# 256-byte alignment, several weight layouts and backward reads in a float32 encoder block

## The chip, the cores and the metric

The kernel runs on one core of one Trainium2 chip. The metric is the device time of one execution in microseconds (us), taken as the median of several runs. A core has five engines that run side by side: TensorE (PE in the profile; its weight loads are PEld), VectorE (DVE), ScalarE (ACT), GpSimd (POOL) and SyncE (SP), which here issues DMAs. They meet through semaphores. Operands lie in SBUF, which has 128 partitions; TensorE writes its results to PSUM.

## The reference

One layer of an encoder block on 512 tokens of width 1024, in float32. Cut to what matters:

```python
h = rms_norm(x, mix_norm_g)
proj = h @ w_in          # mLSTM q,k,v,o,gates | neighbourhood attention q,k,v | memory q | merge gates
y_ml = mlstm_branch(...)             # bidirectional, 4 heads of 128
y_na = neighbourhood_attention(...)  # 8 heads of 64 on an 8 x 64 grid
y_xa = memory_cross_attention(...)   # 4 heads of 128, 256 memory tokens
merged = g_ml * (y_ml @ w_br_ml) + g_na * (y_na @ w_br_na) + g_xa * (y_xa @ w_br_xa)
x = x + merged @ w_out
a, u = split(rms_norm(x, ffn_norm_g) @ w_ffn_up)     # 1024 -> 2 x 2816
x = x + (gelu(dwconv3(a, w_ffn_conv, b_ffn_conv)) * u) @ w_ffn_down
return rms_norm(x, final_norm_g)
```

## The kernel before

Activations are kept with channels on the partitions and the 512 tokens along the free axis. Every large product is done in three matmuls: each operand is split into a high part of type fp32r, a rounded float32, and a low part, which is what is left. `mm3` (L201 to L204) adds high x high (L202), high x low (L203) and low x high (L204) into one PSUM bank. In most products the stationary operand is a 128 x 128 tile of weights and the moving one 128 x 512 of activations; each matmul loads its weights anew.

Weights come in blocks, in one fixed order, `BLOCKS`. `emit_raw` (L141 to L151) starts the DMA of a block into one of three raw buffers, `raw`. `emit_split` (L167 to L188) splits it half by half: ACT copies to the high tile `wh` (L184), DVE subtracts to get the low tile `wl` (L185). There are four buffers for high and four for low tiles, each 544 words wide (`HWD`), so two blocks of two halves fit. `weights` (L190 to L199) hands out a block and sees to it that raw blocks are three ahead and splits one ahead.

`proj` (L332 to L340) is one product over eight steps of k, that is 24 matmuls, into one PSUM bank. The order of stages: mLSTM q and k, the token-major values (256 or 272 columns, activations stationary), memory q and output gates, memory k and v, neighbourhood q and k, then the three branches with their merge gates, with the attention work (generators advanced by `step`) interleaved; then the output projection `out` (activations `GH`, `GL`), and the feed-forward network in two halves of 11. In each half 11 tiles f are made: `ua` (the part that goes through convolution and GELU) and `uu` (the factor), each one block of 8 x 128 columns and 24 matmuls; activations are `HH` and `HL`. Blocks `dn` then do the down projection.

Activations lie in `unit` tiles of 2064 words (`UNIT`), four slices of 512 to a unit; there are 15 of them. Scratch tiles (`scr`) are 516 words wide. Pools lie behind one another: constants, then `wp` (raw, high, low), then the units. Where a tile starts, modulo 256 bytes, follows from these widths.

Of the kernel before, what the change touches and what calls it, by code (L numbers as in the profile page):

```python
# [11 lines left out]
F32 = mybir.dt.float32  # L12
F32R = mybir.dt.float32r
AF = mybir.ActivationFunctionType
ALU = mybir.AluOpType
AX = mybir.AxisListType

P = 128
S = 512
D = 1024  # L20
KT = D // P
# [11 lines left out]
NEG = -1e30  # L33
BW = 1088
HWD = 544
UNIT = 2064
ROWS, GW = 8, 64
CW = (0, 8, 24, 32)
C_ML = (128.0 ** -0.5) / 4.0
# [44 lines left out]
    return L  # L84


BLOCKS = block_list()
BINDEX = {}
_off = 0
# [12 lines left out]
def hybrid_block(ctx, tc, xT, memT, wflat, vecs, gbias, nabias, outa, outb):  # L102
# [14 lines left out]
    def nm(s):  # L117
        uid[0] += 1
        return f"{s}_{uid[0]}"
# [2 lines left out]
        return up.tile([P, UNIT], dt, tag="unit", name=nm("u"))  # L122

    def scr(n=512):
        return sp.tile([P, 516], F32, tag="scr", name=nm("s"))[:, :n]

    def tiny(n):
        return tp.tile([P, 32], F32, tag="tiny", name=nm("y"), bufs=12)[:, :n]
# [8 lines left out]
    raws, split = {}, {}  # L137
# [14 lines left out]
    def halves(i):  # L152
# [2 lines left out]
        k0 = k if n <= HWD else (k + 1) // 2  # L155
        return c, [(0, k0)] + ([(k0, k)] if k0 < k else [])

    lw = []

    def lastw(k, m):  # L160
# [6 lines left out]
    def emit_split(i):  # L167
        key, n = BLOCKS[i]
        r = raws.pop(i)
        c, hs = halves(i)  # L170
        split[i] = []
        for a, b in hs:
            m = (b - a) * c
            if key[0] == "dnl":
                h, l = lastw(4 * key[1] + a, m)
            else:
                h = wp.tile([P, HWD], F32R, tag="hi", name=nm("wh"), bufs=4)
                l = wp.tile([P, HWD], F32R, tag="lo", name=nm("wl"), bufs=4)
            for u, v in ((0, P), (P, m)) if i == 0 and a == 0 else ((0, m),):
                src = r[:, a * c + u:a * c + v]  # L180
                if i == 0 and a == u == 0:
                    V.tensor_copy(h[:, u:v], src)
                else:
                    A.activation(h[:, u:v], src, AF.Copy)  # L184
                V.tensor_tensor(l[:, u:v], src, h[:, u:v].bitcast(F32), op=ALU.subtract)  # L185
            for k in range(a, b):
                q = slice((k - a) * c, (k - a + 1) * c)
                split[i].append((h[:, q], l[:, q]))  # L188

    def weights(key):  # L190

# [17 lines left out]
        V.scalar_tensor_tensor(l, src, scale, h.bitcast(F32), op0=ALU.mult, op1=ALU.subtract)  # L209


    vec = cp.tile([P, NVEC], F32, name="vec")
    gb = cp.tile([P, 16], F32, name="gb")

# [75 lines left out]
    def rstd_row(col, ntok, tag):  # L290

        nt = ntok // P
        ch, cl = tp.tile([P, 32], F32R, tag="tiny", name=nm("y"), bufs=12)[:, :nt], tiny(nt)
        A.activation(ch, col, AF.Copy)
        V.tensor_tensor(cl, col, ch.bitcast(F32), op=ALU.subtract)
        pb = atps()
        for n, c in enumerate((ch.bitcast(F32), cl)):
            dg = sp.tile([P, 516], F32R, tag="scr", name=nm("s"))[:, :ntok]
            for t in range(nt):
                V.tensor_scalar(dg[:, t * P:(t + 1) * P], ident, c[:, t:t + 1], None, op0=ALU.mult)  # L300
            PE.matmul(pb[:, :ntok], onesr, dg, start=n == 0, stop=n == 1)
        rb = cp.tile([P, ntok], F32, name=f"rb_{tag}", tag=f"rb{ntok}", bufs=2 if ntok == S else 1)
        A.activation(rb, pb[:, :ntok], AF.Copy)
        return rb
# [27 lines left out]
    def proj(key, XHs, XLs, n=S, bank=None, at={}):  # L332
        ws = weights(key)
        ps = (bank or mmps)()
        for k in range(KT):
            mm3(ps[:, :n], ws[k][0], ws[k][1], XHs[k], XLs[k], k == 0, k == KT - 1)
            if k in at:
                at[k]()
        return ps
# [73 lines left out]
    for c in range(4):  # L413
        n = 272 if c == 0 else 256
        pss = [(mmps if c % 2 else atps)() for _ in range(NT)]
        for h in range(2):
            ws = weights(("tm", c, h))
            for t in range(NT):
                tsl = slice(t * P, (t + 1) * P)
                for k in range(4):  # L420
                    kk = 4 * h + k
                    ps = pss[t][:, :n]
                    mm3(ps, XH[kk][:, tsl], XL[kk][:, tsl], ws[k][0], ws[k][1], kk == 0, kk == KT - 1)
        for t in range(NT):
            ps = pss[t]
            if c == 0:
                V.scalar_tensor_tensor(Gt[:, t, :], ps[:, :16], rc[:, t:t + 1], gb, op0=ALU.mult, op1=ALU.add)
            if c < 2:
                o = 16 if c == 0 else 0
                A.activation(va[:, t, 2 * c:2 * c + 2, 0:128],  # L430
                             ps[:, o:o + 256].rearrange("p (h c) -> p h c", h=2), AF.Copy, scale=rcc[:, t:t + 1])
            else:

                nv = sp.tile([P, 516], F32R, tag="scr", name=nm("nv"))[:, :512]
                nvv = nv.rearrange("p (q y d) -> p q y d", q=2, y=4)
                pv = ps[:, :256].rearrange("p (q e d) -> p q e d", q=2, e=2)
                A.activation(nvv[:, :, 0:4:3, :], pv, AF.Copy, scale=rc[:, t:t + 1])
                for q in range(2):
                    V.scalar_tensor_tensor(nvv[:, q, 1:3, :], pv[:, q], rc[:, t:t + 1], nvv[:, q, 0:4:3, :].bitcast(F32),
                                           op0=ALU.mult, op1=ALU.subtract)  # L440
                G.dma_start(nav_d[t * P:(t + 1) * P, (c - 2) * 512:(c - 1) * 512], nv)
# [329 lines left out]
    def xa_all(xq, mk, mv, yh, yl):  # L771
        rt = lambda: tp.tile([P, S], F32R, tag="R", name=nm("X"), bufs=4)
        vv = lambda a: a.rearrange("p (m c) -> p m c", m=2)

        def prep(h):
            q, k = (rt(), rt()), rt()
            split_act(q[0], q[1], xq[:, h * S:(h + 1) * S])
            k = (k[:, :M], k[:, M:])
            split_act(k[0], k[1], mk[:, h * M:(h + 1) * M])
            return q, k  # L780

        def prep_v(h):
            v = rt()
            v = (v[:, :M], v[:, M:])
            split_act(vv(v[0]), vv(v[1]), vv(mv)[:, :, h * P:(h + 1) * P])
            return v

        def scores(tq, q, k):
            ps = atps()
            for i in range(2):  # L790
                t = 2 * tq + i
                tsl = slice(t * P, (t + 1) * P)
                mm3(ps[:, i * M:(i + 1) * M], q[0][:, tsl], q[1][:, tsl], k[0], k[1], True, True)
            mx = tiny(2)
            psv = ps.rearrange("p (a b) -> p a b", a=2)
            V.tensor_reduce(mx, psv, axis=AX.X, op=ALU.max, negate=True)
            V.tensor_scalar(mx, mx, XSC, None, op0=ALU.mult)
            sm = scr()
            su = tiny(2)
            for i in range(2):  # L800
                A.activation(sm[:, i * M:(i + 1) * M], psv[:, i, :], AF.Exp, scale=XSC, bias=mx[:, i:i + 1],
                             accum_out=su[:, i:i + 1])
            V.reciprocal(su, su)
            for i in range(2):
                V.tensor_scalar(sm[:, i * M:(i + 1) * M], sm[:, i * M:(i + 1) * M], su[:, i:i + 1], None, op0=ALU.mult)
            return sm

        def transposes(tq, sm, pT):
            pt = atps()
            for i in range(2):  # L810
                for hf in range(2):
                    PE.transpose(pt[:, (2 * hf + i) * P:(2 * hf + i + 1) * P],  # L812
                                 sm[:, i * M + hf * P:i * M + (hf + 1) * P], ident)
            for hf in range(2):
                ms = slice(tq * M, (tq + 1) * M)
                split_act(pT[hf][0][:, ms], pT[hf][1][:, ms], pt[:, hf * M:(hf + 1) * M])

        def values(h, v, pT):
            py = atps()
            for hf in range(2):  # L820
                vs = slice(hf * P, (hf + 1) * P)
                mm3(py, v[0][:, vs], v[1][:, vs], pT[hf][0], pT[hf][1], hf == 0, hf == 1)
            hs = slice(h * S, (h + 1) * S)
            split_act(yh[:, hs], yl[:, hs], py)

        q, k = prep(0)
        yield
        prev = None
        for h in range(4):
            sm = [scores(tq, q, k) for tq in range(2)]  # L830
            if prev:
                values(h - 1, *prev)
            yield
            v = prep_v(h)
            pT = [[sp.tile([P, 516], F32R, tag="scr", name=nm("s"))[:, :S] for _ in range(2)] for _ in range(2)]
            for tq in range(2):
                transposes(tq, sm[tq], pT)
            prev = (v, pT)
            if h < 3:
                q, k = prep(h + 1)  # L840
            yield
        values(3, *prev)
        yield
# [423 lines left out]
```

## Time and profile before

| | |
|---|---|
| three runs | 904.84, 904.88 and 905.72 us, median 904.88 us |
| the profiled execution, first to last instruction | 902.3 us |
| that to the median of the runs | 2.6 us lie outside the span |
| PE busy | 894.4 us (99%), 4438 matmul records |
| PEld busy | 749.2 us (83%) |
| DVE, ACT, POOL busy | 597.7, 464.9, 157.0 us |
| granted TensorE clock, mean | 0.998 |

The page gives for each engine the busy time and its share of the span; the profiled execution's own time is this span and what lies around it, before the first and behind the last instruction. A group of instructions has its line, engine, operation, tiles and shapes, its count, busy time in us and the mean in ns of one, and behind the second bar the idle time before it. [...]

### The profile page before, as it was taken

The page shows a single profiled execution, that of the slowest core. Times are in us where ns is not written, and L with a number is a line of the kernel's source. Part 1 is how long each engine was busy: PE and PEld are TensorE (multiplying, and loading weights), DVE is VectorE, ACT ScalarE, POOL GpSimd, SP SyncE. Part 2 cuts the span into 40 slices and gives each one's busy share as a digit, 9 for nine tenths or more (in the row PEclk, how much of TensorE's full clock was granted, in tenths as well). Part 3 has the DMA queues.
Part 4 walks back from the last instruction along what each step waited for, and adds up shares of the span by engine and source line. Part 5 has one row for each costly group of instructions (what it writes and reads, how often), then busy time and mean ns, then how long its engine had stood idle before and what let it go on. Part 6 is the DMA issues. An engine that isn't in the chain of part 4 may idle for free.

```text
span 902.3 us, 12444 instructions
## 1 busy us (share of the span) xinstructions
PE 894.4 (99%) x4438; PEld 749.2 (83%) x4438; DVE 597.7 (66%) x1138; ACT 464.9 (52%) x982; POOL 157.0 (17%) x236
## 2 busy tenths in 40 slices
PE   9999999999999999999999999999999999999997
PEld 7899888888888888888888888888888888888887
DVE  6795577746566757998766657777733477777433
ACT  7474456656544646898734435444422344444432
POOL 4201231102070660420000211111100011111010
PEclk9999999999999999999999999999999999999999
DMA  8224633422252443443323432222133322222412
GB/s 265 94 76 131 193 134 104 164 94 94 70 136 76 116 126 120 135 135 118 117 88 107 134 108 96 94 98 94 65 99 95 116 94 94 94 93 89 137 33 94
DMA packets 39437, 99.69 MB, mean 110 GB/s; under 512 B 5960, under 2 KB 13640, under 8 KB 39376
## 3 DMA queue, kind: packets, MB, share of 16 engines
q1 hardware_dynamic: 31728, 92.45, 31.2%
q0 software_dynamic: 7360, 6.32, 3.2%
q8 instruction: 35, 0.57, 0.3%
q14 instruction: 26, 0.21, 0.1%
q10 hardware_dynamic: 288, 0.14, 0.1%
HBM read 94.67 MB, written 4.21 MB: 110 GB/s over the span
## 4 chain that ended last, share of the span: by engine, by line
PE 97%; ACT 1%; DMA 1%; issue 1%; SPq 0%; DVE 0%; POOLq 0%; POOL 0%; DVEq 0%
PE mm L202 28%; PE mm L203 28%; PE mm L204 28%; PE at L202 2%; PE at L203 2%; PE at L204 2%; PE at L579 2%; PE at L724 1%; PE at L705 1%; DMA wr<-wflat 1%; PE at L812 0%; PE at L686 0%; PE at L687 0%; ACT s L696 0%; PE at L283 0%
## 5 line engine op out<-in xcount | busy, mean ns | idle before, releaser
L202 PE MATMUL mm<-u,wh 128*128 128x512 f32 (+1 forms) x1077 | 420.3, 390 | 0.8 <-ACT wh L184 0.4
L203 PE MATMUL mm<-u,wh 128*128 128x512 f32 (+1 forms) x1077 | 418.0, 388 | 0.1
L204 PE MATMUL mm<-u,wl 128*128 128x512 f32 (+1 forms) x1077 | 417.3, 387 | 0.0
L184 ACT ACTIVATE wh<-wr 128x512 fp32r<-128x512 f32 (+1 forms) x298 | 185.4, 623 | 249.8 <-PE mm L203 212.8
L185 DVE TENSOR_TENSOR wl<-wr,wh 128x512 fp32r<-128x512 f32 (+3 forms) x299 | 231.3, 775 | 109.0 <-ACT wh L184 102.9
L204 PEld LDWEIGHTS mm<-u,wl 128*128 128x128 f32 x1077 | 202.2, 188 | 44.9 <-DVE wl L185 0.6
L202 PEld LDWEIGHTS mm<-u,wh 128*128 128x128 f32 x1077 | 202.4, 188 | 44.4 <-ACT wh L184 0.9
L203 PEld LDWEIGHTS mm<-u,wh 128*128 128x128 f32 x1077 | 202.5, 188 | 43.4 <-DVE u L209 1.2
L1140 POOL TENSOR_TENSOR s<-s,rb 128x512 f32<-128x512 f32 x22 | 29.1, 1323 | 267.0 <-DVE s L1139 258.9
L451 POOL DMA_DIRECT2D u<-nav_d x128 | 62.2, 506 | 75.2 <-PE at L724 34.4
L208 ACT ACTIVATE u<-s 128x512 fp32r<-128x512 f32 x34 | 21.4, 630 | 53.3 <-DVE s L1143 50.8
L209 DVE SCALAR_TENSOR_TENSOR u<-s,u 128x512 fp32r<-128x512 f32 x34 | 23.5, 692 | 14.9 <-ACT u L208 14.6
L986 POOL TENSOR_TENSOR acc<-acc,s 128x512 f32<-128x512 f32 x7 | 9.1, 1295 | 130.1 <-ACT s L985 130.1
L567 ACT ACTIVATE E<-R,bi 128x128 f32<-128x128 f32 x80 | 28.0, 394 | 7.0 <-POOL R L548 6.5
L369 ACT ACTIVATE s<-pad,vec 128x512 f32<-128x512 f32 x30 | 24.4, 813 | 8.4 <-DVE pad L367 8.4
L370 DVE SCALAR_TENSOR_TENSOR s<-pad,vec,s 128x512 f32<-128x512 f32 x30 | 22.5, 751 | 6.1 <-ACT s L369 6.1
L202 PE MATMUL mm<-wh,u 128*128 128x256 f32 (+1 forms) x80 | 24.5, 307 | 0.0
L203 PE MATMUL mm<-wl,u 128*128 128x256 f32 (+1 forms) x80 | 24.3, 304 | 0.0
L204 PE MATMUL mm<-wh,u 128*128 128x256 f32 (+1 forms) x80 | 24.3, 303 | 0.0
L1139 DVE SCALAR_TENSOR_TENSOR s<-s,s 128x512 f32<-128x512 f32 x22 | 15.2, 692 | 13.4 <-ACT s L1138 13.3
L367 DVE TENSOR_TENSOR pad<-mm,rb 128x512 f32<-128x512 f32 x22 | 15.1, 692 | 12.4 <-PE mm L204 12.4
L371 DVE SCALAR_TENSOR_TENSOR s<-pad,vec,s 128x512 f32<-128x512 f32 x30 | 22.5, 751 | 0.7
(274 smaller groups left out, 1044.7 us busy)
## 6 DMA issues: line engine op xcount, KB each, us to landing
wr<-wflat SPq DMA_DIRECT2D x140, 512.0 KB, 3.4
s<-xT SPq DMA_DIRECT2D x16, 256.0 KB, 4.4
nab<-nabias SPq DMA_DIRECT2D x16, 256.0 KB, 2.7
u<-nav_d POOLq DMA_DIRECT2D x128, 32.0 KB, 2.5
wr<-wflat SPq DMA_DIRECT2D x15, 192.0 KB, 2.4
nav_d<-nv POOLq DMA_DIRECT2D x8, 256.0 KB, 3.1
R<-rd SPq DMA_DIRECT2D x8, 256.0 KB, 3.6
wr<-wflat SPq DMA_DIRECT2D x2, 544.0 KB, 3.3
```

The costliest lines, as they stand in the source:

```text
L184: A.activation(h[:, u:v], src, AF.Copy)
L185: V.tensor_tensor(l[:, u:v], src, h[:, u:v].bitcast(F32), op=ALU.subtract)
L202: PE.matmul(ps, lh, rh, start=start, stop=False)
L203: PE.matmul(ps, lh, rl, start=False, stop=False)
L204: st["mm"] = PE.matmul(ps, ll, rh, start=False, stop=stop).ins
L209: V.scalar_tensor_tensor(l, src, scale, h.bitcast(F32), op0=ALU.mult, op1=ALU.subtract)
L369: A.activation(t1, pad[:, 0:512], AF.Identity, scale=vcol(w, i), bias=vcol(b, i))
L370: V.scalar_tensor_tensor(t1, pad[:, 1:513], vcol(w, n + i), t1, op0=ALU.mult, op1=ALU.add)
L371: V.scalar_tensor_tensor(t1, pad[:, 2:514], vcol(w, 2 * n + i), t1, op0=ALU.mult, op1=ALU.add)
L451: G.dma_start(vw[r * 32:(r + 1) * 32, i * 256:(i + 1) * 256], nav_v[hf, r, CW[b]:CW[b] + 32, hp * 256:(hp + 1) * 256])
L567: A.activation(E[:, i, :], src, AF.Exp, bias=bi[:, d, abs(J - s), s, h:h + 1])
L1140: G.tensor_tensor(c, c, rb2, op=ALU.mult)
```

## The change

It does four things.

1. Widths: a unit becomes 2112 words (8448 bytes, 33 x 256), a scratch tile 512 words, and a tile of 16 words, `edge`, is put ahead of the constants, so that the tiles that TensorE reads start on multiples of 256 bytes.
2. High and low part of a half block share one tile `w` of 1088 words, four buffers of it. Where nothing else is said, the high part starts at word 0 and the low part at word 512 (or 544 for the wider blocks).
3. The blocks of the up projections, `ua` and `uu`, take one of 22 forms in turn, `FORMS`; a form is (step, first word, backwards). Step 1: side by side, the first word 0, 16, 32 or 48. Step 2: high and low interleaved word by word, so that a part takes every second word, the first word a multiple of 8 or 16 up to 56. Step 4: two high and two low parts interleaved, so that a part takes every fourth word. By the order, f = 0, 1, 11 and 12 have step 1, f = 2 to 5 and 13 to 16 step 2, f = 6 and 17 step 4, f = 7, 8, 18 and 19 step 1 backwards, f = 9, 10, 20 and 21 step 2 backwards.
4. Backwards: `proj` reads the activations from token 511 to token 0, and writes PSUM in that order too, so each result lies where it lay before.

The number of matmuls, splits and DMAs stays the same.

```diff
-UNIT = 2064
+WT = 1088
+UNIT = 2112
...
+FORMS = tuple((1, 16 * i, 0) for i in range(4)) + tuple((2, 8 * i, 0) for i in range(8)) + ((4, 0, 0), (4, 16, 0)) \
+    + tuple((1, 16 * i, 1) for i in range(4)) + tuple((2, 16 * i, 1) for i in range(4))
...
-        return sp.tile([P, 516], F32, tag="scr", name=nm("s"))[:, :n]
+        return sp.tile([P, 512], F32, tag="scr", name=nm("s"))[:, :n]
...
+    def layout(key):
+
+        if key[0] in ("ua", "uu"):
+            return FORMS[(2 * key[1] + (key[0] == "uu")) % len(FORMS)]
+        return 1, 0, 0
+
+    def form(w, step, at, m, c):
+
+        if step == 2:
+            e = w[:, at:at + 2 * m].rearrange("p (j x) -> p x j", x=2)
+            h, l = e[:, 0, :], e[:, 1, :]
+        elif step == 4:
+            e = w[:, at:at + 2 * m].rearrange("p (y j z x) -> p x y z j", y=2, x=2, z=2)
+            h, l = e[:, 0], e[:, 1]
+            return h, l, [(h[:, k // 2, k % 2], l[:, k // 2, k % 2]) for k in range(4)]
+        else:
+            h, l = w[:, at:at + m], w[:, WT - m:] if m > 512 else w[:, 512 + at:512 + at + m]
+        q = [slice(k * c, (k + 1) * c) for k in range(m // c)]
+        return h, l, [(h[:, s], l[:, s]) for s in q]
...
-                h = wp.tile([P, HWD], F32R, tag="hi", name=nm("wh"), bufs=4)
-                l = wp.tile([P, HWD], F32R, tag="lo", name=nm("wl"), bufs=4)
+                step, at, _ = layout(key)
+                w = wp.tile([P, WT], F32R, tag="w", name=nm("w"), bufs=4)
+                h, l, parts = form(w, step, at, m, c)
...
+    cp.tile([P, 16], F32, name="edge")
...
-            mm3(ps[:, :n], ws[k][0], ws[k][1], XHs[k], XLs[k], k == 0, k == KT - 1)
+            if layout(key)[2]:
+                mm3(ps[:, ::-1], ws[k][0], ws[k][1], XHs[k][:, ::-1], XLs[k][:, ::-1], k == 0, k == KT - 1)
+            else:
+                mm3(ps[:, :n], ws[k][0], ws[k][1], XHs[k], XLs[k], k == 0, k == KT - 1)
```

More of the change, by code (lines that the diff above doesn't have):

```diff
@@ L175, in emit_split @@
                 h, l = lastw(4 * key[1] + a, m)
+                parts = [(h[:, k * c:(k + 1) * c], l[:, k * c:(k + 1) * c]) for k in range(b - a)]
             else:
-                h = wp.tile([P, HWD], F32R, tag="hi", name=nm("wh"), bufs=4)
-                l = wp.tile([P, HWD], F32R, tag="lo", name=nm("wl"), bufs=4)
+                step, at, _ = layout(key)
+                w = wp.tile([P, WT], F32R, tag="w", name=nm("w"), bufs=4)
+                h, l, parts = form(w, step, at, m, c)
             for u, v in ((0, P), (P, m)) if i == 0 and a == 0 else ((0, m),):
                 src = r[:, a * c + u:a * c + v]
+                if len(h.shape) == 4:
+                    A.activation(h, src.rearrange("p (y z j) -> p y z j", y=2, z=2), AF.Copy)
+                    V.tensor_tensor(l, src.rearrange("p (y z j) -> p y z j", y=2, z=2), h.bitcast(F32), op=ALU.subtract)
+                    continue
                 if i == 0 and a == u == 0:
@@ L185, in emit_split @@
                 V.tensor_tensor(l[:, u:v], src, h[:, u:v].bitcast(F32), op=ALU.subtract)
-            for k in range(a, b):
-                q = slice((k - a) * c, (k - a + 1) * c)
-                split[i].append((h[:, q], l[:, q]))
+            split[i].extend(parts)
     def weights(key):
@@ L297, in rstd_row @@
         for n, c in enumerate((ch.bitcast(F32), cl)):
-            dg = sp.tile([P, 516], F32R, tag="scr", name=nm("s"))[:, :ntok]
+            dg = sp.tile([P, 512], F32R, tag="scr", name=nm("s"))[:, :ntok]
             for t in range(nt):
@@ L432, in hybrid_block @@
             else:
-                nv = sp.tile([P, 516], F32R, tag="scr", name=nm("nv"))[:, :512]
+                nv = sp.tile([P, 512], F32R, tag="scr", name=nm("nv"))[:, :512]
                 nvv = nv.rearrange("p (q y d) -> p q y d", q=2, y=4)
@@ L834, in xa_all @@
             v = prep_v(h)
-            pT = [[sp.tile([P, 516], F32R, tag="scr", name=nm("s"))[:, :S] for _ in range(2)] for _ in range(2)]
+            pT = [[sp.tile([P, 512], F32R, tag="scr", name=nm("s"))[:, :S] for _ in range(2)] for _ in range(2)]
             for tq in range(2):
```

## The prediction

> **What bounds the kernel now.** I read the page first: busy times, the chain that ended last, the costliest groups; then windows over single stages, the timeline of TensorE inside two of them, and the waits.
>
> ```profile
> span 902.3 us, 12444 instructions
> PE 894.4 (99%) x4438; PEld 749.2 (83%) x4438; DVE 597.7 (66%) x1138; ACT 464.9 (52%) x982; POOL 157.0 (17%) x236
> PE 97%; ACT 1%; DMA 1%; issue 1%; SPq 0%; DVE 0%; POOLq 0%; POOL 0%; DVEq 0%
> L202 PE MATMUL mm<-u,wh 128*128 128x512 f32 (+1 forms) x1077 | 420.3, 390 | 0.8 <-ACT wh L184 0.4
> L203 PE MATMUL mm<-u,wh 128*128 128x512 f32 (+1 forms) x1077 | 418.0, 388 | 0.1
> L204 PE MATMUL mm<-u,wl 128*128 128x512 f32 (+1 forms) x1077 | 417.3, 387 | 0.0
> ```
>
> TensorE is the kernel: 99% busy, 97% of the chain, and the idle time before its large groups is under 1 us. Nothing that other engines gain or lose matters until it makes TensorE wait; what counts is the spacing of matmuls. Durations overlap (390 ns long, started every 231 ns), so I go by starts.
>
> ```profile
> 480.00:524.00 44.00, 44.00 (x194) 36.08 (x193) 26.78 (x35) 19.39 (x32) 7.78 (x6) 1.00 0.37 122
> 540.00:660.00 120.00, 120.00 (x519) 97.17 (x518) 88.80 (x125) 55.25 (x88) 14.96 (x11) 1.00 0.29 93
> 665.00:705.00 40.00, 40.00 (x175) 32.52 (x174) 12.82 (x21) 9.49 (x16) 0.00 (x0) 1.00 0.31 102
> 64.00:98.00 34.00, 34.00 (x290) 34.00 (x289) 19.33 (x52) 16.44 (x33) 5.66 (x10) 1.00 0.44 137
> ```
>
> These are stages by window: the output projection, the up projections, the down projection, and a stage with 256-column matmuls; the columns are stretch, length, busy time and count of PE, PEld, DVE, ACT, POOL, granted clock, DMA share and rate. A window counts every matmul that reaches into it, about 1.7 too many at its edges (0.39 long, 0.23 apart). So the spacing is 44/192.3 = 228.8 ns, 120/517.3 = 232.0 ns, 40/173.3 = 230.8 ns, and for 256 columns about 34/289 = 117.6 ns. The clock is 1.00 throughout, so these differences are not the clock.
>
> The same instruction with the same shape thus takes different times by stage. The timeline shows what goes with it:
>
> ```profile
> 503.01 0.39 PE L204 MATMUL mm<-u,wl 128*128 128x512 f32 x1
> 503.23 0.39 PE L202 MATMUL mm<-u,wh 128*128 128x512 f32 x1
> ...
> 505.05 0.40 PE L204 MATMUL mm<-u,wl 128*128 128x512 f32 x1
> 505.28 0.39 PE L202 MATMUL mm<-u,wh 128*128 128x512 f32 x1
> ...
> 508.04 0.40 PE L202 MATMUL mm<-u,wh 128*128 128x512 f32 x1
> ```
>
> From 503.01 to 505.05 lie nine intervals, 226.7 ns each; from there to 508.04 thirteen, 230.0 ns each. This is one accumulation of the output projection, first its k = 0 to 3, then k = 4 to 7. The difference between the halves is where the operands lie. Tiles are laid out in order: three raw buffers of 4352 bytes (17 x 256), four hi and four lo buffers of 2176 (8.5 x 256), then the units of 8256 (32 x 256 + 64). So unit number s lies 64 s bytes off the first modulo 256, and every second hi buffer 128. In the allocation of this program GH and GL of k = 0 to 3 are units 8 and 4, and the weights are in hi and lo buffers 0 or 2: all of them have one remainder modulo 256. For k = 4 to 7 they are units 10 and 1 and buffers 1 or 3: remainders 128, 64 and 128. In the up projections (units 14, 0, 13, 6) they are mixed as well, and the spacing is 232.0. I take it that equal remainders give 226.7 and mixed ones 230 to 232.
>
> **The change part by part.** *Alignment.* A unit becomes 8448 bytes (33 x 256), a weight buffer 4352, a scratch tile 2048, and a 16-word tile rounds the start. Now nearly every operand outside the up projections has one remainder, 0.
>
> ```profile
> L202 PE MATMUL mm<-u,wh 128*128 128x512 f32 x1023 | 405.1, 396 | 0.8 <-ACT wh L184 0.4 <-ACT u L208 0.4
> L202 PE MATMUL at<-u,wh 128*128 128x512 f32 x16 | 6.4, 397 | 0.0
> ```
>
> There are 3 x (1023 + 16) = 3117 such matmuls with stationary weights; 44 blocks of 24, that is 1056, are the up projections, 2061 the rest. Of these 192 are the output projection. Gain: 1869 x (230.8 - 226.7) = 7.7 us, and 192 x (228.8 - 226.7) = 0.4 us: 8.1 us. The equal remainder there was not 0, so the new value is bounded, not seen.
>
> ```profile
> L202 PE MATMUL mm<-u,wh x172: 388/397/398, 540.0 to 659.5; 128*128 128x512 f32 x172
> L203 PE MATMUL mm<-u,wh x172: 387/393/400, 540.3 to 659.7; 128*128 128x512 f32 x172
> L204 PE MATMUL mm<-u,wl x173: 387/392/399, 539.8 to 659.9; 128*128 128x512 f32 x173
> L202 PE MATMUL mm<-u,wh x4: 389/389/395, 502.5 to 504.6; 128*128 128x512 f32 x4
> ```
>
> These are shortest, median and longest durations by line in the up projections, and in the aligned half above. Spacing follows duration (389 goes with 226.7). The shortest seen, 387, would be 224.7: 2061 x 6.1 = 12.6 us gained. The longest, 400, would be 237.7: 2061 x 6.9 = 14 us lost. I take 226.7 because it is the only stretch with equal remainders. The 256-column matmuls (some 630 of the three lines) I leave at 117.6, plus or minus 3 ns, 2 us either way.
>
> *Weight layouts in the up projections.* Each block takes one of 22 forms in turn, so each occurs twice. Side by side: 8 blocks read forwards, with weights 0, 64, 128 or 192 bytes off the activations. Two of them are fully aligned: 48 x (232.0 - 226.7) = 0.3 us gained; the others stay mixed, 0. Interleaved by two (every second word): 16 blocks forwards. Interleaved by four: 4 blocks.
>
> ```profile
> L203 PEld LDWEIGHTS mm<-u,wh 128*128 128x128 f32 x1077 | 202.5, 188 | 43.4 <-DVE u L209 1.2
> ```
>
> What a strided weight load costs no row shows; a load of adjacent words takes 188 ns with its latency. Its bound comes from the 256-column stage, where matmul and load come in pairs every 117.6 ns, so a load keeps its port at most that long. In the up projections a load has 232 ns. It is hidden up to a factor of 1.97, and a gain is excluded, since nothing waits for loads. At one end 0; at the other, at three times (353 ns), 121 ns for each matmul. For the step of two words I take 0 and for four words a factor of two, 235 ns: 96 x 3 = 0.3 us lost. I stay near the lower end because the nearest row has a margin of almost two.
>
> [...]
>
> *Reading backwards.* 16 blocks (f = 7 to 10 and 18 to 21), 384 matmuls, read the activations and write the accumulator from the last column to the first, half of them with the step of two. From below it is 0; a gain is not excluded by more than the 224.7 above (384 x 7 = 3 us). From above: one column costs about (230.8 - 117.6)/256 = 0.44 ns, so at half rate each gains 226 ns, 87 us in all. I take 0, as the same words are read in as regular an order.
>
> *Splitting into strided places.* ACT and DVE now write every second or fourth word.
>
> ```profile
> L184 ACT ACTIVATE wh<-wr 128x512 fp32r<-128x512 f32 x41 | 25.7, 626 | 23.1 <-PE mm L203 23.0
> L185 DVE TENSOR_TENSOR wl<-wr,wh 128x512 fp32r<-128x512 f32 x42 | 36.5, 870 | 5.4 <-ACT wh L184 2.7 <-PE at L301 1.7
> ACT wh L184 <- PE mm L203: 212.8, 162, 2.6
> PE mm L202 <- ACT wh L184: 0.4, 1, 0.4
> ```
>
> The first two rows are of the 540 to 660 window, the others the waits over the whole run. A half is split as soon as its buffer is free, and needed three halves later: 36 x 0.232 = 8.4 us for 0.63 + 0.87 us of work. If all 42 DVE splits there doubled, DVE would be busy 88.8 + 36.5 = 125 of 120 us, and the cover would be gone; but only 28 of 44 blocks are strided, which gives 88.8 + 23 = 112. Cost 0. Hi and lo now share a tile: the buffer comes free with the L204 matmul in place of L203, 0.23 us later, inside those 8.4 us. What queues behind the waiting ACT split is the GELU chain, whose results wait for a later down projection. At the very start a matmul may wait for the low part too, at most one DVE split, 0.9 us; I take 0.
>
> Sum: -8.1 - 0.3 + 0.3 = -8.1 us on the span of 902.3, so 894.2. The three runs have a median of 904.88, 2.6 us outside the span; so 896.8 us.
>
> **The rivals.**
> *Forecast* (0.50): as above, 890 to 901.
> *Larger gain* (0.06): the aligned spacing is 224.7 and the interleaved blocks profit too: 3117 x 6.5 = 20 us, 885. For it: shortest durations of 387 occur in all stages; against: the only aligned stretch never goes below 389.
> *Alignment alone doesn't do it* (0.11): the 226.7 came from something else than equal remainders. Then the spacing stays, and what remains are small costs: 903 to 908. For it: only some ten matmuls per block in one stage have it. Against: it returns in all eight blocks of that stage.
> *Backward reading slows the matmul* (0.16): at half rate 87 - 8 = 79 us slower, 984; where a quarter of the rate is lost, 384 x 57 = 22 us, 919. It decides as soon as one backward matmul costs 21 ns more (8.1/384). For it: no row of before has TensorE running downwards; against: the words lie as close together as before, and a stage whose activations come in short runs has no slower matmuls than others:
>
> ```profile
> L686 PE MATMUL at<-KS,QS 128*128 128x256 f32 x32 | 8.5, 285 | 0.0
> L202 PE MATMUL mm<-u,u 128*128 128x256 f32 x44 | 12.9, 293 | 0.0
> ```
>
> The first reads eight runs of 32 columns, the second 256 in a row.
>
> *The strided load becomes the bound* (0.17): with 232 ns available it starts to pay from a factor of 1.97. At 2.5 (294 ns) for both steps 672 x 62 = 42 us less 8, 939; at three times for the step of four alone 96 x 121 = 11.6 less 8, 908. For it: PEld is already 83% busy; against: those 188 ns include latency, since loads of the same length come every 117.6 ns in the 256-column stage.
>
> [...]
>
> **How the numbers follow.** A measurement tells 0.2%, 1.8 us, from no change. Faster: 0.50 + 0.06 = 0.56. Alignment without effect is split, 0.07 same and 0.04 slower; with the last two rivals slower is 0.37. For 8 in 10 the range goes from 884, the larger gain, to 939; beyond it lie the heavier halves of the last two rivals, some 0.17, and 0.02 below. The likeliest case's own range is 890 to 901.
>
> **What would show it.** Right: PE still near 99%; in the down projection 40 us hold 176.5 matmuls at 226.7, and L202 to L204 there have a median of 389. PEld in the up projections stays hidden: the spacing in blocks f = 2 to 5 (step of two) is 226 to 233, in f = 6 (step of four) under 240. In f = 7 to 10 and 18 to 21 the spacing is like that of f = 2 to 5. Wrong: a spacing of 250 or more in the backward blocks, PEld longer than 188 by more than 110 ns where weights are interleaved, L185 over 1.4 us with TensorE waiting on DVE, or an unchanged 230.8 in the down projection.

## The result and the profile after

After the change the kernel takes 899.12 us (median of three runs, 897.81 to 899.35), before 904.88 us: a ratio of 0.9933, interval [0.9914, 0.9953]. The profiled execution took 899.35 us, with a span of 897.6 us, 4.7 us less than before. The change makes the kernel faster, by 0.67%, in the forecast's direction, and lands 2.3 us above its number.

The page of the changed kernel, busy times, the chain that ended last and the costliest groups:

```profile
span 897.6 us, 12396 instructions
PE 888.7 (99%) x4438; PEld 758.9 (85%) x4438; DVE 599.7 (67%) x1138; ACT 467.6 (52%) x982; POOL 158.0 (18%) x236
PE 93%; ACT 2%; DMA 2%; DVE 2%; issue 1%; SPq 0%; POOL 0%; POOLq 0%; ACTq 0%; DVEq 0%
L229 PE MATMUL mm<-u,w 128*128 128x512 f32 (+1 forms) x1077 | 418.7, 389 | 1.1 <-ACT w L213 0.8
L230 PE MATMUL mm<-u,w 128*128 128x512 f32 (+1 forms) x1077 | 416.2, 386 | 0.1
L231 PE MATMUL mm<-u,w 128*128 128x512 f32 (+1 forms) x1077 | 416.2, 386 | 0.0
```

`mm3` now has its matmuls in L229 to L231 and the splits are in L213 (ACT) and L214 (DVE). TensorE is still 99% busy and nearly never waits; the counts are the same. Only PEld has grown, by 9.7 us, and none of it shows as idle time of PE. As before, the spacing by stage is what tells. The windows of the changed kernel, with the columns and the edge correction of the prediction (1.7 matmuls too many; 2.4 in the last row, where a matmul of 283 ns starts every 120):

```profile
477.10:520.60 43.50, 43.50 (x193) 36.03 (x192) 26.30 (x35) 18.95 (x32) 7.77 (x6) 1.00 0.37 123
544.10:588.60 44.50, 44.50 (x193) 37.39 (x192) 33.45 (x51) 23.65 (x36) 7.96 (x5) 1.00 0.29 95
588.60:599.90 11.30, 11.30 (x49) 11.30 (x49) 8.97 (x12) 5.67 (x9) 1.29 (x1) 1.00 0.30 95
600.00:622.30 22.30, 22.30 (x97) 17.99 (x96) 16.00 (x22) 10.24 (x17) 2.94 (x2) 1.00 0.29 95
622.40:644.60 22.20, 22.20 (x97) 18.55 (x96) 17.02 (x22) 10.24 (x17) 2.58 (x2) 1.00 0.24 68
652.30:704.70 52.40, 52.40 (x233) 43.39 (x232) 18.43 (x28) 12.64 (x21) 0.00 (x0) 1.00 0.33 110
64.00:98.00 34.00, 34.00 (x285) 34.00 (x285) 19.09 (x52) 16.07 (x32) 5.67 (x10) 1.00 0.43 140
```

From the top: output projection 43.5/191.3 = 227.4 ns (before 228.8); up projections with step two 44.5/191.3 = 232.6; with step four 11.3/47.3 = 239; read backwards side by side 22.3/95.3 = 234, backwards with step two 22.2/95.3 = 233; down projection 52.4/231.3 = 226.5 (before 230.8); the 256-column stage 34/282.6 = 120.3 (before, by the same correction, 34/287.6 = 118.2). The granted clock is 1.00 in all of them. The three short windows are up to 1% off: by the starts of the matmuls themselves step four stands at 236.5 ns and both backward groups at 233.3. So alignment pays in the stages that it reaches with 512 columns, the up projections pay a little for each layout, and the 256-column stage, which was aligned too, got slower.

The same by groups of instructions, each from the stage of its own (down projection, step two, step four, backwards side by side); the last number before the second bar is the mean duration in ns:

```profile
L231 PE MATMUL mm<-u,w 128*128 128x512 f32 x78 | 30.3, 389 | 0.0
L231 PE MATMUL mm<-u,w 128*128 128x512 f32 x65 | 25.6, 394 | 0.0
L229 PE MATMUL mm<-u,w 128*128 128x512 f32 x16 | 6.4, 399 | 0.0
L229 PE MATMUL mm<-u,w 128*128 128x512 f32 x31 | 12.3, 397 | 0.0
```

A duration is the spacing and some 162 to 164 ns: 389 goes with 226.7, 394 with 232, 397 with 233.3, 399 with 236.5. So a mean duration read from a group already tells the spacing to a nanosecond or two.

The weight loads in the windows of step two, of step four and of side by side (backwards), and the splits into places with a step of two:

```profile
L231 PEld LDWEIGHTS mm<-u,w 128*128 128x128 f32 x62 | 12.1, 195 | 2.3
L231 PEld LDWEIGHTS mm<-u,w 128*128 128x128 f32 x16 | 5.0, 310 | 0.0
L231 PEld LDWEIGHTS mm<-u,w 128*128 128x128 f32 x31 | 5.8, 188 | 1.4
L214 DVE TENSOR_TENSOR w<-wr,w x13: 682/686/689, 548.0 to 579.0; 128x512 fp32r<-128x512 f32 x13
L213 ACT ACTIVATE w<-wr x13: 648/663/687, 544.7 to 578.2; 128x512 fp32r<-128x512 f32 x13
```

Step two costs a load 7 ns and step four about 120. The DVE split is not slower at step two (686 ns median; 684 in a stretch of the up projections before), the ACT split by some 6% (663 against 626). None of that reaches TensorE. Its waits over the whole run:

```profile
PE mm L229 <- ACT w L213: 0.8, 1, 0.8
PE at L610 <- DVE E L600: 0.4, 1, 0.4
PE at L755 <- DVE w L744: 0.3, 1, 0.3
```

The first is at the start (0.4 before), the second is new, in the attention work.

Summing the distances from start to start by kind of matmul in both traces says where the 4.7 us came from. The 512-column matmuls outside the up projections gain 7.8 us, the first wait left out; the 272-column ones and the 13 on the tile `warm` at the start gain 0.2 together. Those of the up projections lose 0.75, the 630 of 256 columns lose 1.0 (119.3 to 121.0 ns on average), the first wait is 0.4 longer, and the small matmuls of the attention lose 1.1, about half of it at the wait at L610 and half at a wait at L755 (one distance between its matmuls is 620 ns, where before none was over 225).

### The profile page after: what moved, and what is told of

It reads as the page before. It is cut to its first block, busy times and chain, and to the rows that moved or that the text cites. A ratio compares the mean times of both kernels' runs of the same rounds, so it can differ in the third digit from the quotient of the medians.

```text
span 897.6 us, 12396 instructions
## 1 busy us (share of the span) xinstructions
PE 888.7 (99%) x4438; PEld 758.9 (85%) x4438; DVE 599.7 (67%) x1138; ACT 467.6 (52%) x982; POOL 158.0 (18%) x236
## 4 chain that ended last, share of the span: by engine, by line
PE 93%; ACT 2%; DMA 2%; DVE 2%; issue 1%; SPq 0%; POOL 0%; POOLq 0%; ACTq 0%; DVEq 0%
PE mm L229 27%; PE mm L231 27%; PE mm L230 27%; PE at L229 2%; PE at L231 2%; PE at L230 2%; PE at L610 2%; PE at L755 1%; DMA R<-rd 1%; PE at L736 1%; DMA wr<-wflat 1%; DMA rd<-s 0%; PE at L843 0%; ACT s L727 0%; PE at L717 0%
## 5 line engine op out<-in xcount | busy, mean ns | idle before, releaser
L229 PE MATMUL mm<-u,w 128*128 128x512 f32 (+1 forms) x1077 | 418.7, 389 | 1.1 <-ACT w L213 0.8
L230 PE MATMUL mm<-u,w 128*128 128x512 f32 (+1 forms) x1077 | 416.2, 386 | 0.1
L231 PE MATMUL mm<-u,w 128*128 128x512 f32 (+1 forms) x1077 | 416.2, 386 | 0.0
L213 ACT ACTIVATE w<-wr 128x512 fp32r<-128x512 f32 (+1 forms) x290 | 181.9, 631 | 239.1 <-PE mm L231 207.0
L214 DVE TENSOR_TENSOR w<-wr,w 128x512 fp32r<-128x512 f32 (+3 forms) x291 | 220.8, 760 | 116.7 <-ACT w L213 113.4
L231 PEld LDWEIGHTS mm<-u,w 128*128 128x128 f32 x1077 | 207.7, 193 | 39.8 <-DVE w L214 0.4
L229 PEld LDWEIGHTS mm<-u,w 128*128 128x128 f32 x1077 | 207.8, 193 | 39.4 <-ACT w L213 1.3
L230 PEld LDWEIGHTS mm<-u,w 128*128 128x128 f32 x1077 | 207.8, 193 | 38.8 <-DVE u L236 0.8
L229 PE MATMUL mm<-w,u 128*128 128x256 f32 (+1 forms) x80 | 24.7, 308 | 0.0
L231 PE MATMUL mm<-w,u 128*128 128x256 f32 (+1 forms) x80 | 24.4, 305 | 0.0
L230 PE MATMUL mm<-w,u 128*128 128x256 f32 (+1 forms) x80 | 24.3, 304 | 0.0
L1169 ACT ACTIVATE s<-s 128x512 f32<-128x512 f32 x22 | 13.9, 632 | 17.0 <-DVE s L1168 16.9
```

The lines of the kernel that those rows point to most:

```text
L229: PE.matmul(ps, lh, rh, start=start, stop=False)
L230: PE.matmul(ps, lh, rl, start=False, stop=False)
L231: st["mm"] = PE.matmul(ps, ll, rh, start=False, stop=stop).ins
```

## The experiments

The theory to test: the spacing of a matmul is set by the remainders modulo 256 bytes of what is read, equal ones giving 226.7 ns, and each layout of the up projections costs what the windows show and no more. Rivals: that multiples of 256, not equal remainders, matter; that the price is paid per column, or in the weight load; that backward costs only together with certain layouts.

**All blocks side by side, forwards** (`e1_all_flat`): the alignment of the change without its layouts.

```diff
     def layout(key):
 
-        if key[0] in ("ua", "uu"):
-            return FORMS[(2 * key[1] + (key[0] == "uu")) % len(FORMS)]
         return 1, 0, 0
```

> The changed kernel with every block of the up projections side by side from word 0 and read forwards; so all large products have equal remainders modulo 256. Theory A (equal remainders give one fixed spacing, 226.7 ns for 512 columns): the up projections go from about 232.3 to 226.7, 1056 x 5.6 = 5.9 us less than the changed kernel, about 893.2 us, and L229 to L231 have a median of 389 ns there. Rival B (the up projections are slow for another reason, such as their DVE load): their spacing stays above 230 and the time stays at 899.

892.1 us, ratio to before 0.9854 [0.9839, 0.9869], span 890.4; the kernel before beside it took 905.37. A window in the up projections, 540 to 640, in this run:

```profile
540.00:640.00 100.00, 100.00 (x443) 82.80 (x442) 72.64 (x109) 48.15 (x79) 16.73 (x10) 1.00 0.29 93
```

100/441.3 = 226.6 ns where before had 232.0. So alignment alone gives over twice the gain of the change (13.3 us against 5.8), and the layouts take about half of it back. Summed from start to start, the 1056 matmuls of the up projections take 245.8 us in the changed kernel and 239.5 here: 6.3 us are the price of the layouts. The spans differ by 7.2; the other 0.9 are the first wait, 0.35 shorter here, and the wait at L610, which is absent here.

**All blocks backwards, side by side** (`e2_all_backward`):

```diff
-        if key[0] in ("ua", "uu"):
-            return FORMS[(2 * key[1] + (key[0] == "uu")) % len(FORMS)]
-        return 1, 0, 0
+        return 1, 0, int(key[0] in ("ua", "uu"))
```

> As e1, but all blocks of the up projections side by side from word 0 and read backwards (f = 0 keeps its own forward loop). Theory A with a fixed price for backward reading (233.3 ns for each, seen in the changed kernel): 1008 x 6.6 = 6.7 us more than e1, about 899.9 us. Rival (the backward blocks were slow because they came mixed with other layouts): equal to e1.

899.81 us, 0.9933 [0.9916, 0.995], span 898.1. The same window:

```profile
540.00:640.00 100.00, 100.00 (x430) 80.55 (x430) 75.47 (x106) 47.06 (x76) 14.28 (x10) 1.00 0.28 92
```

100/428.3 = 233.5 ns, by the starts 233.3. All tiles start at remainder 0 here, as in the run before, and yet each backward matmul costs 6.6 ns more than a forward one. The two blocks of f = 0 have a forward loop of their own, so 1008 matmuls pay: 1008 x 6.6 = 6.7 us, which is also what the starts sum up to. The spans differ by 7.7; the other 1.0 us lies ahead of the 256-column stage, at the start of the kernel. Nothing like half rate, and not free either. What is not told apart: a backward read begins at its last word, 252 bytes behind a multiple of 256, so the 6.6 ns may belong to the direction or to that place; no run reads backwards with the weights at the same remainder.

**All operands 64 bytes off** (`e3_all_at_64`): the run `e1_all_flat` with

```diff
-    cp.tile([P, 16], F32, name="edge")
+    cp.tile([P, 32], F32, name="edge")
```

> As e1, but the tile ahead of the constants is 32 words wide, so that every operand lies 64 bytes behind a multiple of 256. Theory A (equal remainders): the same time as e1, 893.2 us, spacing 226.7. Rival C (multiples of 256 bytes themselves): spacing back at 230 to 233 and 2 to 5 ns more for each of 3117 matmuls, 900 to 907 us.

892.09 us, 0.9852 [0.9837, 0.9867]. The group of the up projections, 560 to 640:

```profile
L227 PE MATMUL mm<-u,w 128*128 128x512 f32 x119 | 46.3, 389 | 0.0
```

389 ns once more. Equal remainders do it; that the starts lie on multiples of 256 does nothing here (892.09 us against 892.1).

**Units of 2112 words in the kernel before** (`e4_units_only`): activations aligned among each other, weights still at 0 or 128.

```diff
-UNIT = 2064
+UNIT = 2112
```

> The kernel before with units of 2112 words alone: all activations have one remainder, the weights of k = 0 to 3 the same one, those of k = 4 to 7 lie 128 bytes off (two of the four buffers). Theory A: k = 0 to 3 at 226.7, k = 4 to 7 at about 232 (the changed kernel's blocks with weights 128 off), 229.5 on average, 3117 x 1.8 = 5.6 us less than before, about 899.3 us. Rival C (multiples of 256): as before, 904.9. Rival D (it is enough that the activations are alike): 226.7 throughout, about 891 us.

902.62 us, 0.9972 [0.9959, 0.9985], span 900.8: a gain of 2.5 us by the ratio and 1.5 on the span. That lies between theory A (899.3) and C (904.9) and far from D (891). The reason stands in the timeline of this run, in one block of the output projection. Up to k = 3 its weights have the remainder of the activations; from 489.1 on they lie 128 bytes off:

```profile
486.34 0.40 PE L202 MATMUL mm<-u,wh 128*128 128x512 f32 x1
...
487.96 0.39 PE L203 MATMUL mm<-u,wh 128*128 128x512 f32 x1
...
488.64 0.39 PE L203 MATMUL mm<-u,wh 128*128 128x512 f32 x1
...
491.89 0.40 PE L202 MATMUL mm<-u,wh 128*128 128x512 f32 x1
```

The first seven intervals are 231.4 ns although the remainders are equal, then come three of 226.7, then fourteen of 232.1, the first two of them still in k = 3. After a stretch with unequal remainders it takes up to eight matmuls in this run until the short spacing is back (seven in the output projection, three in most of the up projections' blocks with equal remainders), and two in the output projection of the kernel before. Where equal and unequal stretches of twelve alternate, as in this stage, the equal ones average 229.8 and the unequal ones 233.0, so that the stage is slower than before (231.2 against 229.1). The remainder alone, taken matmul by matmul, is therefore only half of the rule; what went before counts as well.

**The price by itself** (`p1_price_by_itself`): `e1_all_flat` with 14 series of 33 independent matmuls behind the output projection, one property changed in each; their results are not used.

```diff
+    series("qa")                      # 512 columns, 128 x 128 weights, all aligned
+    series("qb", n=384)
+    series("qc", n=256)
+    series("qd", m=64)                # 64 weight columns
+    series("qe", m=32)
+    series("qf", wt=0)                # one weight column repeated
+    series("qg", mv=-1)               # activations read backwards
+    series("qh", out=-1)              # PSUM written backwards
+    series("qi", mv=-1, out=-1)
+    series("qj", wt=2)                # weights with a step of two
+    series("qk", mv=2)                # activations with a step of two
+    series("ql", mv=4)
+    series("qm", m=64, mv=-1)
+    series("qn", m=32, mv=-1)
```

> e1 with 14 series of 33 matmuls added between the output projection and the feed-forward network; their results are not used. Operands lie at multiples of 256 bytes; a series differs from the first, qa (512 columns, 128 weight columns), in one thing. [...] Rival B (one sixteenth on top of every column): qb 170.0, qc 113.3, qd, qe and qf 226.7. Backwards: qg reads activations backwards, qh writes the accumulator backwards, qi does both; if the reading is the price, qg and qi 233.3 and qh 226.7; if the writing is, qh and qi 233.3 and qg 226.7. qj has weights in every second word: 233 (as in the changed kernel). [...]

1011.92 us with the series in it. Its timeline, one row for each series; the spacing is the distance to the next row's start, divided by the count:

```profile
527.75 4.49 PE L1037 MATMUL qa<-u,u 128*128 128x512 f32 x19
532.08 5.39 PE L1037 MATMUL qb<-u,u 128*128 128x384 f32 x30
537.30 3.75 PE L1037 MATMUL qc<-u,u 128*128 128x256 f32 x30
540.89 7.30 PE L1037 MATMUL qd<-u,u 128*64 128x512 f32 x31
548.02 7.82 PE L1037 MATMUL qe<-u,u 128*32 128x512 f32 x33
555.67 7.80 PE L1037 MATMUL qf<-u,u 128*128 128x512 f32 x33
563.32 7.87 PE L1037 MATMUL qg<-u,u 128*128 128x512 f32 x33
571.03 7.67 PE L1037 MATMUL qh<-u,u 128*128 128x512 f32 x33
578.53 7.87 PE L1037 MATMUL qi<-u,u 128*128 128x512 f32 x33
586.24 7.86 PE L1037 MATMUL qj<-u,u 128*128 128x512 f32 x33
593.93 15.11 PE L1037 MATMUL qk<-u,u 128*128 128x512 f32 x33
608.86 15.40 PE L1037 MATMUL ql<-u,u 128*128 128x512 f32 x33
624.08 7.88 PE L1037 MATMUL qm<-u,u 128*64 128x512 f32 x33
```

Within the series, away from their ends and at a granted clock of 1.00, that settles at 226.7 (qa), 173.3 (384 columns), 120.0 (256 columns), 230.1 and 231.7 (64 and 32 weight columns), 231.7 (one column repeated), 233.3 (read backwards, qg and qi, and with 64 and 32 weight columns, qm and qn), 226.7 (written backwards, qh), 233.3 (weights with a step of two, qj), 453.3 and 461.3 (activations with a step of two and of four). Four things follow. Aligned, the spacing is N x 0.4167 + 13.3 ns for all three widths: at equal remainders the price is a fixed one for each matmul, not one per column (170.0 and 113.3 would have been that). It isn't a price per weight word either: a quarter of the weights makes it 231.7, not less. Of the backward blocks, the reading pays and the writing is free. And a step of two in the activations doubles the matmul, where the same step in the weights costs 6.6 ns.

So the same step costs differently by who reads. A weight load takes 195 ns at step two and 310 at step four, 188 side by side; a matmul goes from 226.7 ns to 453.3 at step two of its activations and to 461.3 at step four; VectorE's split, which reads the high part and writes the low one in every second word, takes 686 ns, and 684 with adjacent words. Why these differ was not tested.

**Weights 0, 32, ... 224 bytes off** (`p2_offsets`): 16 such series on `e1_all_flat`, eight with 512 columns and eight with 256; their results are not used.

```diff
+    for j, off in enumerate((0, 8, 16, 24, 32, 40, 48, 56)):
+        series("ra rb rc rd re rf rg rh".split()[j], off=off)
+    for j, off in enumerate((0, 8, 16, 24, 32, 40, 48, 56)):
+        series("sa sb sc sd se sf sg sh".split()[j], n=256, off=off)
```

> e1 with 16 series of 33 matmuls added at the same place, results not used: ra to rh have 512 columns and the weights 0, 32, 64, ... 224 bytes behind the remainder of the activations, sa to sh the same with 256 columns. Theory A (equal remainders are the best place for 512 columns): ra 226.7, the others 228 to 234. Rival (some other distance is better): one of them under 226. For 256 columns, where the aligned kernel has 120.0 and the mixed one 117.6, some distance lies under 118; if all lie at 120, the gain of the mixed kernel came from elsewhere.

988.93 us. At 512 columns the settled spacings are 226.7, 233.3, 233.3, 234.5, 232.4, 233.3, 228.9 and 233.3 ns: 0 is best. At 256 columns they are 120.0, 118.3, 113.3, 120.0, 118.8, 120.0, 117.8 and 117.8: 0 is among the worst, and the best is 64 bytes. Four rows of the timeline (weights 0, 32, 64 and 96 bytes off, 256 columns):

```profile
585.25 4.11 PE L1037 MATMUL sa<-u,u 128*128 128x256 f32 x33
589.20 4.07 PE L1037 MATMUL sb<-u,u 128*128 128x256 f32 x33
593.10 3.93 PE L1037 MATMUL sc<-u,u 128*128 128x256 f32 x33
596.87 4.12 PE L1037 MATMUL sd<-u,u 128*128 128x256 f32 x33
```

33 matmuls take 3.95, 3.90 and 3.77 us; the 0.18 us between sa and sc is 5.5 ns for each, 6.7 once settled. That is why the 256-column stages lose by alignment: before, their remainders were mixed and some lay well. The 113.3 ns are 256 x 0.4167 and one sixteenth more, the number that a price per column would give, as 226.7 is at 512. So the fixed 13.3 ns are what equal remainders showed, not a price for every distance: at 64 bytes 256 columns have 6.6 above 256 x 0.4167. What they are stays open.

**Three remainders at once** (`p3_triples`): 64 series of twelve triples as `mm3` has them; high activations at 0, low activations, high and low weights each at 0, 64, 128 or 192 bytes; results not used.

> e1 with 64 series tabc of 12 triples (high x high, high x low, low x high, 512 columns) added at the same place, results not used. High activations lie at remainder 0, low activations 64 a bytes behind, high weights 64 b, low weights 64 c. Theory A (all alike is the best place): t000 226.7 and all others 228 to 238. Rival (the shortest spacings of the kernel before, 224 ns between unlike remainders, can be had steadily): some series stays under 226 in its last six triples.

1427.38 us. All four alike (t000) is the only one at 226.7:

```profile
521.05 0.39 PE L1025 MATMUL t<-u,u 128*128 128x512 f32 x1
...
525.59 0.39 PE L1027 MATMUL t<-u,u 128*128 128x512 f32 x1
```

Twenty intervals of 227.0 in the series' first part. The next best, six of the 64, settle at 228.9 to 229.1; 28 stand at 231.1 or 233.3, the worst at 235.5. None is below 226: for 512 columns nothing better than all alike was found, among steps of 64 bytes.

**The stationary operand 64 bytes off, for 256 columns alone** (`e5_256_at_64`): what the offsets point to, on `e1_all_flat`, in 516 of the 630 matmuls.

```diff
+        if key[0] == "tm" and key[1] > 0:
+            return 1, 48, 0
+        if key[0] == "dn" and key[1] == 1 and key[2] == LF - 1:
+            return 1, 16, 0
-        return 1, 0, 0
+        return 1, 16 if key[0] == "memk" else 0, 0
...
-        q = slice(k % 8 * 256, k % 8 * 256 + m)
+        q = slice(16 + k % 8 * 256, 16 + k % 8 * 256 + m)
```

> e1 with the weights of three groups of 256-column products moved so that the stationary operand lies 64 bytes behind the moving one (values of c = 1 to 3, memory keys, halves of the last output tiles); in the last 66 matmuls, where roles are swapped, it lies 192 behind. The offset series gave 113.3 ns at 64, 117.8 at 192 and 120.0 at 0. Theory (the distance of the two addresses modulo 256 sets the spacing): 288 + 96 + 132 = 516 matmuls lose 6.7 ns and 66 lose 2.2, 3.6 us less than e1, about 888.5 us. Rival (the 113.3 belongs to the series alone, where every operand keeps its distance): less than 1.2 us less than e1.

889.65 us, 0.9831 [0.9815, 0.9848], span 887.7. Since that is only 2.5 us from `e1_all_flat`, which ran on another chip, both ran once more side by side:

> The kernel of e1 once more, beside that of e5 on one chip, to tell the two apart: about 892 us.

> The kernel of e5 beside that of e1. If the distance of 64 bytes is worth what the 256-column stage showed (113.3 in place of 120.0 for 288 matmuls, 1.9 us, and the other groups), 2 to 4 us less than e1; if the difference of the earlier calls was one between chips, under 1 us.

Flat 892.89 us (0.9871 [0.9854, 0.9887]), with the 64 bytes 889.44 (0.983 [0.9815, 0.9845]): 3.45 us apart, 2.5 in the spans. The windows of the 256-column stage, flat first:

```profile
64.00:96.00 32.00, 32.00 (x269) 32.00 (x268) 17.46 (x46) 14.30 (x29) 4.79 (x9) 1.00 0.43 136
64.00:96.00 32.00, 32.00 (x283) 31.96 (x282) 18.65 (x49) 15.76 (x32) 5.67 (x10) 1.00 0.47 150
```

32/266.6 = 120.0 against 32/280.6 = 114.0 ns; 516 x 6 = 3.1 us, between the two differences; summed from start to start the 630 matmuls take 2.9 us less. This is the fastest version found, 9.7 us below the changed kernel by the medians (0.983 against 0.9933 of the kernel before beside each).

## Why the prediction was right, point by point

*Bound.* Right: PE stayed at 99% and the spacing decided.

*Alignment outside the up projections, -8.1 us.* Right in reason and nearly in size: measured -7.8 us, of it -7.5 for the 2061 matmuls that it counted, and the sign named for it came (226.5 ns in the down projection, mean duration 389). The rule behind it was too simple, though. Equal remainders give 226.7 only once they have lasted for some matmuls, up to eight in `e4_units_only`. It came out because the change makes everything around equal too.

*256-column matmuls, 0.* Mis-sized: measured +1.0 us, inside the 2 us allowed. The step that failed is to leave them alone because no row showed them aligned; `p2_offsets` shows that 0 is a bad distance for them, and `e5_256_at_64` that the good one is worth some 3 us. The 117.6 itself was a little low: with 2.4 matmuls taken off for the edges of the window, not one, it is 118.2.

*Two aligned blocks and side by side, -0.3.* The two blocks do run at 226.6 and 227.5; the others stand at 229.1 to 233.2 depending on the offset (64, 128, 192 bytes), so that "the others stay mixed, 0" was fair.

*Step of two, 0.* Right: 229.9 to 233.6 by block, within the 226 to 233 that was named but for 0.6 ns.

*Step of four, +0.3.* The two positions of these blocks stand at 235.0 and 238.0, under the 240 that was named. The factor of two behind the +0.3, like the 2.5 and three of the rival, was an assumption that no run shows; the runs showed loads of 195 ns at step two and 310 at step four against 188, factors of 1.04 and 1.65. The sign given for "wrong", a load longer by more than 110 ns, came true and meant little: about 120 ns longer, some 4.5 ns of it in the spacing, 0.4 us in all. That threshold should have been set on the spacing, since loads of 310 ns still run beside matmuls 235 apart. The time of the rival (939 or 908) did not come.

*Reading backwards, 0.* Mis-sized: 233.3 against 232, 1.4 ns x 384 = 0.5 us. Its reason was wrong, since "the same words in as regular an order" does cost, 6.6 ns for each matmul against an aligned forward one (by the direction or by where the read begins); it is hidden in this change because the up projections stood at 232 anyhow. Its price was to be 21 ns before the rival decided. Nothing in the runs is near half rate for backward reading; half rate exists (453.3 ns), but for the step of two in activations, which the change doesn't have.

*The other rivals.* That alignment alone doesn't do it fell with `e1_all_flat`; the larger gain from a spacing of 224.7 fell with `p3_triples`, where nothing came below 226, though 13.3 us were there to be had, by leaving the layouts out.

*Price of a column.* The 0.44 ns per column came from two windows with unequal alignment; with both aligned it is (226.7 - 120.0)/256 = 0.417, and 13.3 ns per matmul come on top.

*Splits, 0.* Right: DVE unchanged at 686, ACT 6% longer, and no wait behind them in the up projections.

*Start, 0 (at most 0.9).* +0.4, from 0.4 to 0.8, as the first wait for ACT. But this wait changes from one execution to the next: `e1_all_flat` and `e6_flat_beside` are one program, and it is 0.5 us in the first and absent in the second. The wait at L610 (0.5 us from start to start) wasn't in the sum; it, too, comes and goes. `p1_price_by_itself` and `p3_triples` are the same program up to there, and only the second has it (p1 first, idle time behind the second bar):

```profile
L608 PE MATMUL at<-u,E 128*128 128x129 f32 x160 | 20.5, 275 | 0.0
L608 PE MATMUL at<-u,E 128*128 128x129 f32 x160 | 20.8, 276 | 0.4 <-DVE E L598 0.4
```

So these 0.9 us can't be laid to the change. The 0.5 us at L755 wasn't in the sum either; `e1_all_flat` and `e6_flat_beside` both have it (620 and 606 ns from start to start). Its cause was not tested and stays open.

So the 3.4 us by which the span came out above the forecast (897.6 against 894.2) are 1.0 for the 256-column term, 0.75 for the up projections, 0.3 for the main term, 0.4 for the first wait and 1.1 for the attention; the 272-column matmuls and those on `warm` give back 0.2.

*From the span to the median, +2.6.* Wrong, and it helped. Where a run has both its span and its time, 1.7 to 1.8 us lie outside the span (here 897.6 and 899.35). By that, the profiled execution of the kernel before took about 904.1 us, less than each of the three runs. With 1.8 the forecast would have been 896.0 and the miss 3.1 us in place of 2.3, so a part of that nearness is luck.

## What to carry to other kernels

Measure the start-to-start distance of matmuls by stage before anything else: in the kernel before it differed by 3 ns in 230 between stages of the same shape, at full clock, and aligning the tiles alone was worth 1.5%. Put all operands of a run of 512-column fp32r matmuls at one remainder modulo 256 bytes, for the whole run and not for half of it (226.7 ns alike, 228.9 to 235.5 otherwise in `p2_offsets` and `p3_triples`; 229.8 in the equal stretches that alternate in `e4_units_only`), and test other widths by themselves: 256 columns were best at another distance (113.3 ns at 64 bytes, 120.0 at 0). A layout that is hidden, as interleaved weights or backward reading here, can still take back what alignment gives (6.3 us here), so try the alignment alone first.

## What the runs showed of the hardware that was not expected

- At equal remainders a matmul costs N x 0.4167 + 13.3 ns for 256, 384 and 512 columns (120.0, 173.3, 226.7); a quarter of the weight columns makes it 231.7, not less. What the 13.3 ns are stays open.
- The best distance between stationary and moving operand is 0 bytes at 512 columns (226.7, else up to 234.5) and 64 at 256 columns (113.3, else up to 120.0). Why these differ is not settled.
- The spacing has a memory: in the output projection of `e4_units_only` seven intervals of 231.4 passed at equal remainders before 226.7 was back.
- Reading activations backwards costs 6.6 ns (233.3 against 226.7), whatever the weight layouts tried; whether by the direction or by the place where the read begins is open. Writing PSUM backwards costs nothing (226.7). A step of two words in the activations doubles the matmul (453.3), and lengthens even the load beside it:

```profile
L1037 PEld LDWEIGHTS qk<-u,u x33: 188/207/209, 593.7 to 608.0; 128*128 128x128 f32 x33
```

These are weights of adjacent words, loaded beside activations with a step of two: the load has a median of 207 ns, 19 more than the 188 beside the aligned forward activations of qa; why was not tested.
